# SBUF pools moved to two sides, rounded operands behind a 32-byte pad, in a two-block transformer kernel

## Chip, cores and metric

The kernel runs on one core of a Trainium2 chip, in one launch. The metric is device time in microseconds (us), the median of several runs. It holds two transformer blocks on 256 tokens with a model width of 1024, all in float32.

## What is computed

The first block normalises `x`, projects it, runs two attentions side by side (differential attention and a low-rank latent attention), gates and merges them, and adds a SwiGLU feed-forward layer. The second block does this twice: feed-forward, a mixer (retention the first time, stick-breaking attention the second), feed-forward, and a gated embedding. Nearly all the work is products with weight matrices:

```python
h = rms_norm(x, ln_mix_pre); z = h @ w_in
...                                   # two attentions on slices of z
merged = sigmoid(g_a) * (oa @ w_proj_a) + sigmoid(g_b) * (ob @ w_proj_b)
x = x + rms_norm(merged @ w_o, ln_mix_post)
x = x + rms_norm((silu(h @ w_gate) * (h @ w_up)) @ w_down, ln_ffn_post)
...                                   # second block, for i in (0, 1):
h = h + 0.5 * rmsnorm(swiglu(rmsnorm(h), gate, up, down))
h = h + rmsnorm(retention(rmsnorm(h)) if i == 0 else stick_breaking(rmsnorm(h)))
h = h + 0.5 * rmsnorm(swiglu(rmsnorm(h), gate, up, down))
h = h + rmsnorm(sigmoid(rmsnorm(h) @ ple_w_gate) * (p[i] @ ple_w_proj))
```

## The kernel before

**Rounded pairs.** Each float32 operand of a weight product is split into a rounded high part and a rounded rest, both of type float32r, and a product is three matmuls: high by high, high by rest, rest by high. `chunk` (line 161) loads up to 2048 columns of weights into a `w_raw` tile (a DMA on SP's queue, line 176), ScalarE rounds them into `w_hi` in pieces of 512 columns (line 188) and VectorE subtracts to get `w_lo` (line 189). A 512-column piece is 2,048 bytes in each partition. The activations are kept the same way: `x_hi` and `x_lo` (the input of a stage), `a_hi` and `a_lo` (the hidden layer of a feed-forward stage), `oa`, `ob`, `m` (the attention outputs and their merge), `u` (retention), `o` (stick-breaking), `pe` (the embedding input).

**Which operand moves.** A matmul has a stationary operand of 128 columns, loaded first, and a moving operand that streams past it. In `mm3` (line 192, its matmuls recorded as line 197), which `tokens` and `token_steps` call, the activation is stationary and 512 columns of weights move; one activation tile serves as `x[0]`, `x[0]`, `x[1]`, so a triple reads the high tile twice and the low tile once as stationary operands. In `mat_steps` (matmuls recorded as line 214) it is the other way round: 128 weight columns are stationary and 256 token columns of the activation move. The trace writes a matmul as out<-moving,stationary.

**Stages.** `first` runs the first block's mixer; `ffn` runs gate and up (activation `x`) and then, through `end_stage`, down (activation `a`, 22 row tiles, 2 token halves, 2 column halves: 88 triples for each of 5 stages). TensorE executes in program order; the loads run ahead over 3 `w_raw` buffers and 12 buffers each of `w_hi` and `w_lo`.

**Where tiles lie.** SBUF memory is given out by pools. A pool takes a stretch of every partition when it opens and gives it back when it closes; the tiles in it are rounded up to 32 bytes. All pools here are on the left side: they are stacked upwards from byte 16,512 of the partition in the order in which they open. From the tiles' sizes the places are: `const` 16,512, `raw` 20,448, `hip` (all `w_hi`) 45,024, `lop` (all `w_lo`) 69,600, `act` 94,176 with `h` first (8,192 bytes), `x_hi` at 102,368 and `x_lo` at 110,560, then `sm` 118,752 and `tmp` 123,008. `ob_hi` and `ob_lo` take the places of `x_hi` and `x_lo` (same tags in `act`). Above, from 136,320, come the pools that live for a stage: `mix` (with `oa`, `va`, `vb`, `m`, `cq`, `ckv`), `big0`, then `p_halves` (for good), and on top of it `big0a`, `ret_u` and `ret`, `emb0` and `big0b` and so on.

**Remainders of these places.** Divided by 64, the places of `w_raw`, `w_hi`, `w_lo`, `h`, `x` and `ob` leave 32. All the tiles in the stage pools (`a`, `u`, `oa`, `m`, `o`, `pe`, `cq`, `ckv`, and retention's `p` and `v`) leave 0. Divided by 512, `w_hi`, `w_lo`, `x` and `ob` leave 480 and the stage tiles named leave 128. Slices inside a tile start at multiples of 512 bytes, so every operand of a float32r weight product has its tile's remainder.

Of the kernel before, what the change touches and what calls it, by code (L numbers as in the profile page):

```python
# [10 lines left out]
F32 = mybir.dt.float32  # L11
# [7 lines left out]
P = 128  # L19
T = 256  # L20
D = 1024
# [73 lines left out]
class Weights:  # L95


    def __init__(self):
        self.parts = []
# [45 lines left out]
class Build:  # L145
    def __init__(self, ctx, tc, aps):
        self.ctx, self.tc, self.nc = ctx, tc, tc.nc
        self.aps = aps
        self.plan = []
        self.at = 0  # L150
        pool = lambda name, bufs, **k: ctx.enter_context(tc.tile_pool(name=name, bufs=bufs, **k))
        self.const = pool("const", 1)
        self.raw = pool("raw", 3)
        self.hip = pool("hip", WB)
        self.lop = pool("lop", WB)
        self.act = pool("act", 1)
        self.sm = pool("sm", 2)
        self.tmp = pool("tmp", 2)
        self.psm = pool("psm", 4, space=PSUM)
        self.psa = pool("psa", 4, space=PSUM)  # L160
        self.filler, self.behind, self.late = Filler(), None, []
        self.later = None
# [337 lines left out]

    def setup(self):
        nc, const, aps = self.nc, self.const, self.aps
        self.h = self.act.tile([P, 2, D], F32, name="h", tag="h")

        self.h0 = self.h.rearrange("p b d -> p (b d)").rearrange("p (k t) -> p k t", k=KT)
        self.vecs = const.tile([P, NV], F32, name="vecs")
        self.kc = const.tile([P, NK], F32, name="kc")
        nc.scalar.dma_start(self.kc[:, :P], aps["kc"][:, :P])
        nc.scalar.dma_start(self.vecs[:, :KT], aps["vecs"][:, :KT])
        self.pos = self.tmp.tile([P, T], I32, name="pos", tag="s")  # L510
        self.lam = self.tmp.tile([P, 4 * 64], F32, name="lam", tag="s")
        self.ident = self.kc[:, K_ID : K_ID + P]
        self.ones = const.tile([P, P], F32, name="ones")
        nc.vector.memset(self.ones, 1.0)
        self.dummies(WARM[0])
        self.mhalf = const.tile([P, 2], F32, name="mhalf")
        nc.vector.memset(self.mhalf, -0.5)
# [777 lines left out]
    def run(self):  # L1295
        tc = self.tc
        self.setup()
        g2 = lambda i, n: self.vec(V_G2 + (i * 8 + n) * 8, 8)
        row = lambda i, n: R_G2 + 4 * i + n // 2
        stage = self.first()  # L1300
        with tc.tile_pool(name="big0", bufs=1) as self.big:
            self.ffn(*stage, ("w_ffn_gate", "w_ffn_up", "w_ffn_down"), (0,), R_FFN, 1.0)
        names = ("ffn_w_gate_2", "ffn_w_up_2", "ffn_w_down_2")
        out = self.aps["out"].rearrange("p (b d) -> p b d", b=2)
        p_halves = self.ctx.enter_context(tc.tile_pool(name="p_halves", bufs=1))
        self.pe = [p_halves.tile([P, SUB], F32R, name=f"pe_{x}") for x in "hl"]
        pos = self.tmp.tile([P, T], I32, name="pos", tag="s")
        self.nc.gpsimd.dma_start(pos, self.aps["pos2"].to_broadcast([P, T]))
        self.table2 = self.rope_table("2", pos, self.kc[:, K_F2 : K_F2 + 1], self.const)
        for i in range(2):  # L1310
            with tc.tile_pool(name=f"big{i}a", bufs=1) as self.big:
                self.ffn(*self.next_stage(g2(i, 0)), names, (i, 0), row(i, 1), 4.0)
            self.later = lambda i=i: self.embed_in(i)
            mixer = self.stick if i else self.retention
            mixer(*self.next_stage(g2(i, 2)), row(i, 3))
            with tc.tile_pool(name=f"emb{i}", bufs=1) as emb:
                e = emb.tile([P, 2, D], F32, name="e")
                self.embed(i, e)
                with tc.tile_pool(name=f"big{i}b", bufs=1) as self.big:
                    self.ffn(*self.next_stage(g2(i, 4)), names, (i, 1), row(i, 5), 4.0)  # L1320
                self.ple(i, *self.next_stage(g2(i, 6), 4.0), e, row(i, 7), out if i else None)
        assert self.at == WCOLS * P, (self.at, WCOLS * P)
# [66 lines left out]
```

## Time and profile before

| | |
|---|---|
| median of 3 runs | 1613.9 us (1613.33 to 1614.34) |
| the profiled execution, its own time | 1613.39 us |
| its span (first to last instruction) | 1611.5 us |
| mean granted TensorE clock | 0.998 |
| TensorE matmul, weight load | 99%, 83% of the span |
| VectorE, ScalarE, GpSimd | 66%, 56%, 5% of the span |

The profile is one execution of the program. In its lists PE is TensorE's matmuls and PEld its loads of stationary operands, which overlap the matmuls; DVE is VectorE, ACT ScalarE, POOL GpSimd, SP the queue that issues most DMAs. The duration of a matmul in a list runs until its last result is written, so matmuls that follow each other overlap; the time one costs is read from start to start. The order of the work is on TensorE's queue, so the profile is read in three steps: the chain of work that ended last, the list of groups, and then single stages in order of time.

### The profile page before, as it was taken

How to read it: one execution, taken by the hardware profiler on the slowest of the kernel's cores; microseconds unless marked ns; L12 is line 12 of the kernel's file. 1: busy time of each engine (PE TensorE's matmuls, PEld its weight loads, DVE VectorE, ACT ScalarE, POOL GpSimd, SP SyncE). 2: the span in 40 equal slices, each digit the busy share in tenths (PEclk: the TensorE clock that was granted, in tenths of full speed). 3: DMA queues.
4: the chain of work that ended last, by engine and by line, in shares of the span. 5: the costliest groups of instructions: out<-in, count | busy, mean ns of one | idle time of the engine just before them, and what ended most of it. 6: DMA issues, size and time to landing. Idle time of an engine off the chain costs nothing.

```text
span 1611.5 us, 22515 instructions
## 1 busy us (share of the span) xinstructions
PE 1597.7 (99%) x8230; PEld 1344.3 (83%) x8230; DVE 1065.2 (66%) x1969; ACT 904.1 (56%) x1792; POOL 79.9 (5%) x97
## 2 busy tenths in 40 slices
PE   9999999999999999999999999999999999999997
PEld 8898778888888888898888888878888899888886
DVE  7987766765566665777766555486665677666546
ACT  6665544755455554645546555476554656655545
POOL 0000000200001000100000000012000200000001
PEclk9999999999999999999999999999999999999999
DMA  7535436455546555555455555555555554455552
GB/s 243 211 123 190 167 106 221 183 179 201 183 159 220 183 183 183 167 189 183 160 190 179 187 178 188 183 198 200 183 183 183 176 192 149 165 183 183 183 175 73
DMA packets 47134, 288.72 MB, mean 179 GB/s; under 512 B 5968, under 2 KB 9168, under 8 KB 14384
## 3 DMA queue, kind: packets, MB, share of 16 engines
q1 hardware_dynamic: 44528, 279.29, 49.3%
q0 software_dynamic: 2064, 7.80, 1.4%
q8 instruction: 64, 1.05, 0.3%
q14 instruction: 46, 0.38, 0.1%
q10 hardware_dynamic: 432, 0.20, 0.0%
HBM read 284.78 MB, written 1.05 MB: 177 GB/s over the span
## 4 chain that ended last, share of the span: by engine, by line
PE 95%; DVE 2%; DMA 1%; issue 1%; ACT 1%; SPq 0%; POOL 0%; POOLq 0%; DVEq 0%; ACTq 0%
PE ps L197 78%; PE ps L214 9%; PE at L628 1%; PE S L660 1%; PE xt L429 1%; DMA w_raw<-in_w 1%; DVE w_lo L189 1%; PE o L197 1%; PE o L707 0%; DMA h<-in_x 0%; PE S L1073 0%; PE S L1187 0%; PE pt L697 0%; PE o L834 0%; PE ot L1110 0%
## 5 line engine op out<-in xcount | busy, mean ns | idle before, releaser
L189 DVE TENSOR_TENSOR w_lo<-w_raw,w_hi 128x512 fp32r<-128x512 f32 x1054 | 708.8, 687 | 348.8 <-ACT w_hi L188 343.5
L188 ACT CAST w_hi<-w_raw 128x512 fp32r<-128x512 f32 x1054 | 639.6, 621 | 489.2 <-PE ps L197 355.8
L197 PE MATMUL ps<-w_hi,x_hi 128*128 128x512 f32 (+1 forms) x1280 | 488.9, 382 | 0.3 <-ACT x_hi L433 0.3
L197 PE MATMUL ps<-w_hi,x_lo 128*128 128x512 f32 (+1 forms) x1280 | 483.0, 377 | 0.5 <-DVE x_lo L435 0.5
L197 PE MATMUL ps<-w_lo,x_hi 128*128 128x512 f32 (+1 forms) x1280 | 482.1, 377 | 0.0
L197 PEld LDWEIGHTS ps<-w_hi,x_lo 128*128 128x128 f32 x1280 | 240.8, 188 | 46.9 <-DVE x_lo L435 2.1
L197 PEld LDWEIGHTS ps<-w_hi,x_hi 128*128 128x128 f32 x1280 | 241.0, 188 | 43.3 <-issue 1.0
L197 PEld LDWEIGHTS ps<-w_lo,x_hi 128*128 128x128 f32 x1280 | 241.2, 188 | 42.1
L197 PE MATMUL ps<-w_hi,a_hi 128*128 128x512 f32 x440 | 176.7, 402 | 0.0
L197 PE MATMUL ps<-w_hi,a_lo 128*128 128x512 f32 x440 | 173.3, 394 | 0.0
L197 PE MATMUL ps<-w_lo,a_hi 128*128 128x512 f32 x440 | 172.6, 392 | 0.0
L296 POOL TENSOR_TENSOR r<-v,mhalf 128x1 f32<-128x1 f32 (+1 forms) x50 | 61.4, 1228 | 1262.6 <-DVE v L384 1097.7
L214 PE MATMUL ps<-x_hi,w_hi 128*128 128x256 f32 x440 | 114.8, 289 | 0.7 <-ACT x_hi L356 0.5
L214 PE MATMUL ps<-x_hi,w_lo 128*128 128x256 f32 x440 | 112.5, 284 | 0.6 <-DVE w_lo L189 0.6
L197 PEld LDWEIGHTS ps<-w_hi,a_lo 128*128 128x128 f32 x440 | 82.6, 188 | 21.3
L197 PEld LDWEIGHTS ps<-w_lo,a_hi 128*128 128x128 f32 x440 | 82.7, 188 | 19.2
L197 PEld LDWEIGHTS ps<-w_hi,a_hi 128*128 128x128 f32 x440 | 82.6, 188 | 18.4
L214 PEld LDWEIGHTS ps<-x_hi,w_hi 128*128 128x128 f32 x440 | 84.0, 191 | 2.2 <-issue 0.7
L214 PEld LDWEIGHTS ps<-x_hi,w_lo 128*128 128x128 f32 x440 | 84.1, 191 | 1.5 <-DVE w_lo L189 1.2
L623 DVE SCALAR_TENSOR_TENSOR a<-ps,R,s 128x512 f32<-128x512 f32 (+1 forms) x60 | 42.2, 703 | 55.4 <-PE ps L197 44.0
L214 PE MATMUL ps<-x_lo,w_hi 128*128 128x256 f32 x440 | 77.4, 283 | 0.0
L270 ACT CAST a_hi<-at 128x512 fp32r<-128x512 f32 (+1 forms) x60 | 33.1, 551 | 70.4 <-PE at L628 70.4
(271 smaller groups left out, 1484.0 us busy)
## 6 DMA issues: line engine op xcount, KB each, us to landing
w_raw<-in_w SPq DMA_DIRECT2D x254, 1024.0 KB, 4.9
gr<-in_rows POOLq DMA_DIRECT2D x10, 512.0 KB, 4.1
w_raw<-in_w SPq DMA_DIRECT2D x7, 512.0 KB, 3.4
w_raw<-in_w SPq DMA_DIRECT2D x12, 256.0 KB, 5.1
w_raw<-in_w SPq DMA_DIRECT2D x6, 384.0 KB, 3.3
h<-in_x SPq DMA_DIRECT2D x4, 256.0 KB, 5.6
h<-in_x POOLq DMA_DIRECT2D x1, 1024.0 KB, 8.9
out<-h SPq DMA_DIRECT2D x3, 256.0 KB, 2.5
```

Of the source, the lines that this page charges most:

```text
L188: nc.scalar.copy(hi[:, :m], r[:, c0:c1])
L189: nc.vector.tensor_sub(lo[:, :m], r[:, c0:c1], hi[:, :m].bitcast(F32))
L197: mm = lambda a, b, **k: nc.tensor.matmul(ps, a, b, skip_group_check=True, **k)
L214: mm = lambda *a, **k: self.nc.tensor.matmul(*a, skip_group_check=True, **k)
L270: nc.scalar.copy(hi, src)
L296: self.nc.gpsimd.tensor_tensor(r, v, self.mhalf[:, :n], op=ALU.pow)
L429: nc.tensor.transpose(pt[:, i, :], self.h[:, b, k * P : (k + 1) * P], self.ident)
L623: nc.vector.scalar_tensor_tensor(a, banks[1], R[:, b : b + 1], s, op0=ALU.mult, op1=ALU.mult)
L628: nc.tensor.transpose(pt[:, i, :], a[:, i * P : (i + 1) * P], self.ident)
L660: mm(S[:, at], q[:, qs], k[:, ks], start=n == 0, stop=n == len(parts[0]) - 1, skip_group_check=True)
```

## The change

Pools get a side. `const`, `raw`, `sm`, `tmp`, later `p_halves` and `emb0`/`emb1` go to the right side, where pools are stacked downwards from byte 229,344; `h` moves out of `act` into a pool `res` of its own on the right. On the left a pool `pad` with one tile of 8 floats (32 bytes) opens first, so that `hip`, `lop`, `act` and the stage pools are stacked from byte 16,544. No instruction on any engine is written, removed or given other shapes; the pad is never read or written.

```diff
-        self.const = pool("const", 1)
-        self.raw = pool("raw", 3)
+
+        self.const = pool("const", 1, side="right")
+        self.raw = pool("raw", 3, side="right")
+        pool("pad", 1).tile([P, 8], F32, name="pad")
         self.hip = pool("hip", WB)
         self.lop = pool("lop", WB)
         self.act = pool("act", 1)
-        self.sm = pool("sm", 2)
-        self.tmp = pool("tmp", 2)
+        self.res = pool("res", 1, side="right")
+        self.sm = pool("sm", 2, side="right")
+        self.tmp = pool("tmp", 2, side="right")
...
-        self.h = self.act.tile([P, 2, D], F32, name="h", tag="h")
+        self.h = self.res.tile([P, 2, D], F32, name="h", tag="h")
...
-        p_halves = self.ctx.enter_context(tc.tile_pool(name="p_halves", bufs=1))
+        p_halves = self.ctx.enter_context(tc.tile_pool(name="p_halves", bufs=1, side="right"))
...
-            with tc.tile_pool(name=f"emb{i}", bufs=1) as emb:
+            with tc.tile_pool(name=f"emb{i}", bufs=1, side="right") as emb:
```

## Rows read from the trace of the kernel before

**Rows 1.** The page's head: span, and each engine's busy time.

```profile
span 1611.5 us, 22515 instructions
PE 1597.7 (99%) x8230; PEld 1344.3 (83%) x8230; DVE 1065.2 (66%) x1969; ACT 904.1 (56%) x1792; POOL 79.9 (5%) x97
```

**Rows 2.** The page's chain that ended last, shares by engine and by line.

```profile
PE 95%; DVE 2%; DMA 1%; issue 1%; ACT 1%; SPq 0%; POOL 0%; POOLq 0%; DVEq 0%; ACTq 0%
PE ps L197 78%; PE ps L214 9%; PE at L628 1%; PE S L660 1%; PE xt L429 1%; DMA w_raw<-in_w 1%; DVE w_lo L189 1%; PE o L197 1%; PE o L707 0%; DMA h<-in_x 0%; PE S L1073 0%; PE S L1187 0%; PE pt L697 0%; PE o L834 0%; PE ot L1110 0%
```

**Rows 3.** Timeline, TensorE, a gate/up stage: start us, duration us, matmul.

```profile
339.75 0.39 PE L197 MATMUL ps<-w_hi,x_hi 128*128 128x512 f32 x1
...
349.95 0.39 PE L197 MATMUL ps<-w_hi,x_hi 128*128 128x512 f32 x1
```

**Rows 4.** Timeline, TensorE, the down stage that follows it.

```profile
429.75 0.40 PE L197 MATMUL ps<-w_hi,a_hi 128*128 128x512 f32 x1
429.99 0.39 PE L197 MATMUL ps<-w_lo,a_hi 128*128 128x512 f32 x1
430.22 0.39 PE L197 MATMUL ps<-w_hi,a_lo 128*128 128x512 f32 x1
...
439.55 0.40 PE L197 MATMUL ps<-w_hi,a_hi 128*128 128x512 f32 x1
```

**Rows 5.** Timeline, TensorE, end of the second attention's projection and start of w_o.

```profile
261.54 0.39 PE L197 MATMUL ps<-w_hi,ob_hi 128*128 128x512 f32 x1
...
263.58 0.39 PE L197 MATMUL ps<-w_hi,ob_hi 128*128 128x512 f32 x1
...
268.65 0.39 PE L197 MATMUL ps<-w_hi,m_h 128*128 128x512 f32 x1
...
271.45 0.39 PE L197 MATMUL ps<-w_hi,m_h 128*128 128x512 f32 x1
```

**Rows 6.** Timeline, TensorE, retention's output products of one head.

```profile
768.88 0.39 PE L197 MATMUL o<-v_l,p_h 128*128 128x512 f32 x1
...
769.58 0.39 PE L197 MATMUL o<-v_h,p_l 128*128 128x512 f32 x1
...
770.27 0.39 PE L197 MATMUL o<-v_h,p_l 128*128 128x512 f32 x1
```

**Rows 7.** Busy time of each engine in that down stage (PE, PEld, DVE, ACT, POOL; clock, DMA).

```profile
418.00:474.00 56.00, 56.00 (x242) 45.06 (x241) 27.97 (x42) 25.99 (x44) 0.55 (x1) 1.00 0.54 188
338.00:356.00 18.00, 18.00 (x81) 14.87 (x80) 10.12 (x15) 9.64 (x16) 0.00 (x0) 1.00 0.60 208
```

**Rows 8.** Groups of matmuls by shape: counts | busy us, mean ns | idle before.

```profile
L197 PE MATMUL ps<-w_hi,x_hi 128*128 128x512 f32 x1120 | 442.9, 395 | 0.3 <-ACT x_hi L433 0.3
L197 PE MATMUL ps<-w_hi,a_hi 128*128 128x512 f32 x440 | 176.7, 402 | 0.0
L197 PE MATMUL ps<-w_hi,u_h 128*128 128x512 f32 x64 | 25.1, 392 | 0.0
L197 PE MATMUL ps<-w_hi,m_h 128*128 128x512 f32 x32 | 12.7, 398 | 0.0
L197 PE MATMUL ps<-w_hi,pe_h 128*128 128x512 f32 x16 | 6.3, 392 | 0.0
L197 PE MATMUL o<-v_h,p_h 128*128 128x512 f32 x12 | 4.6, 421 | 0.0
L197 PE MATMUL ps<-w_hi,ckv_h 128*128 128x512 f32 x8 | 3.3, 408 | 0.0
L214 PE MATMUL ps<-x_hi,w_hi 128*128 128x256 f32 x440 | 114.8, 289 | 0.7 <-ACT x_hi L356 0.5 <-DVE h L774 0.2
L197 PE MATMUL ps<-w_hi,x_hi 128*128 128x256 f32 x160 | 46.0, 288 | 0.0
L214 PE MATMUL ps<-cq_h,w_hi 128*128 128x256 f32 x36 | 9.9, 296 | 0.0
```

**Rows 9.** Timeline, TensorE, 256-column matmuls, moving operand x, then cq.

```profile
681.45 0.28 PE L214 MATMUL ps<-x_hi,w_hi 128*128 128x256 f32 x1
...
682.89 0.28 PE L214 MATMUL ps<-x_hi,w_hi 128*128 128x256 f32 x1
...
165.79 0.28 PE L214 MATMUL ps<-cq_h,w_hi 128*128 128x256 f32 x1
...
167.90 0.28 PE L214 MATMUL ps<-cq_h,w_hi 128*128 128x256 f32 x1
```

**Rows 10.** Groups by shape: the two largest of the transposes.

```profile
L628 PE MATMUL at<-kc,a 128*128 128x128 f32 x220 | 33.7, 271 | 0.0
L429 PE MATMUL xt<-kc,h 128*128 128x128 f32 x144 | 19.9, 274 | 0.5 <-DVE h L415 0.5
```

**Rows 11.** Groups by shape, VectorE: the subtraction that makes w_lo.

```profile
L189 DVE TENSOR_TENSOR w_lo<-w_raw,w_hi 128x512 fp32r<-128x512 f32 x1042 | 702.7, 689 | 348.2 <-ACT w_hi L188 342.9
```

## Prediction

> **What bounds the kernel now.** First read the page's head: matmuls keep TensorE busy for 1597.7 of 1611.5 us, VectorE 66%, ScalarE 56% [rows 1]. Then the chain that ended last: TensorE holds 95% of it, and 78% is one line, the 512-column matmuls of line 197 [rows 2]. So a wait removed on another engine is worth almost nothing here; what counts is how long TensorE takes from one matmul to the next. The change alters no instruction, only where operands lie. So the third look is at single stages, from start to start, and the question is whether that time already differs between places.
>
> It does. In a gate/up stage 45 matmuls start between 339.75 and 349.95: 10.20 us, 0.680 a triple, 227 ns each [rows 3]. In the down stage that follows, same line, same shapes, 42 matmuls take from 429.75 to 439.55: 9.80 us, 0.700 a triple, 233 ns each [rows 4]. Both run at a granted clock of 1.00 (the 2.4 GHz level), and TensorE never goes idle in either stretch [rows 7], so neither clock nor starvation makes the difference. The stationary operand does differ: `x` leaves 32 divided by 64, `a` leaves 0. A cleaner pair: near the end of the second attention's projection, with `ob` in `x`'s place, 9 matmuls take 2.04 us (0.680 a triple); just after, in w_o, with `m` in a stage pool, 12 take 2.80 us (0.700) [rows 5]. Line, moving buffers, shapes and neighbours in time are alike; only the stationary tile's place is another. And it isn't that stationary and moving tile must match: retention's `p` and `v` both leave 128 divided by 512, and six of their matmuls take 1.39 us, 232 ns each [rows 6], nearer to 233 than to 227, though six are few. So I read a stationary operand's place as costing 6.7 ns a matmul (20 ns a triple) where it leaves 0.
>
> **Where everything goes.** By the pools' sizes: on the left the pad at 16,512, `w_hi` from 16,544, `w_lo` from 41,120, `x_hi` 65,696, `x_lo` 73,888, the stage pools from 82,080. Every tile of rounded operands on the left is a multiple of 512 bytes long, so all of them there leave 160 divided by 512, 32 divided by 64. `a`, `u`, `oa`, `m`, `o`, `cq`, `ckv`, `p` and `v` thus go from 0 to 32; `w`, `x`, `ob` stay at 32. On the right: `const` 225,408 (each constant keeps its remainder by 64), `raw` 200,832 (32 becomes 0), `h` 192,640 (32 becomes 0), `tmp` 175,072, `p_halves` 170,976 (0 becomes 32), `emb` 162,784. The largest stage pool, `mix`, ends at 169,120, so all fits.
>
> **The gain.** Triples whose stationary operand leaves 0 today: 440 with `a`, 64 with `u`, 32 each with `oa`, `m` and `o` (the row of `m` stands for three), 16 with `pe`, 12 with `p`, 8 with `ckv` [rows 8]: 636. At 0.700 - 0.680 = 0.020 us that is 12.7 us. The load that costs is, as I read it, that of the next matmul's stationary operand, so where another kind of matmul follows (a transpose after a triple, at the ends of runs) nothing is gained; I take off 0.3 us for some 45 such places: 12.4.
>
> Does it reach the end? These stages are TensorE back to back. In 56 us of a down stage VectorE is busy 27.97 and ScalarE 25.99 us, DMA 0.54 [rows 7]; a stage 3% shorter asks 3% more of each, and the gate/up stage already runs at the faster pace with VectorE at 10.12 of 18 us. So all of it.
>
> **The losses.** As moving operand `cq` (remainder 0) is a little faster today than `x` (32): 18 matmuls of 256 columns in 2.11 us, 117 ns, against 12 in 1.44 us, 120 ns [rows 9]. `cq` (3 x 36 matmuls) and `ckv` (3 x 16) go to 32: 156 x 2.8 ns = 0.4 us lost. Transposes: 220 of `a` last 271 ns, 144 of `h` 274 ns [rows 10], and the two swap remainders: (220 - 144) x 3 ns = 0.2 us at most, either way; I take 0. The float32 matmuls of the attentions are not told apart by any row; their lines hold some 2% of the chain [rows 2], 32 us, and 3% of that (what 20 ns is of 0.700 us) is 1 us either way; I take 0.
>
> `w_raw` changes its remainder, which could change ScalarE's rounding or VectorE's subtraction (689 ns [rows 11]) and the DMA's writes; no row shows either at another place. VectorE, the busier of the two, has a third of its time free [rows 1], so its subtraction could be a third longer (10.12 us would become some 13 of 18 [rows 7]) before TensorE waited: 0. If that cover went, the price would be set by the stage: every per cent by which VectorE outlasted TensorE is a per cent of that stage. At the start, some 40 us fed by DMA, and where stages change, a shifted place may release a buffer sooner or later: `emb`'s tile no longer shares memory with the stage before it. In the chain DMA and VectorE together hold 3%, 48 us [rows 2], so a tenth of that, 5 us, bounds it both ways; nothing waits on `e` on the chain, I take 0.
>
> Sum: 12.4 - 0.4 = 12.0 us. The profiled execution took 1613.39 us (its span 1611.5, 1.9 around it), 0.5 below the median of 1613.9. 1613.39 - 12.0 = 1601.4; on the median's scale 1601.9. I forecast 1602.
>
> **What the Trainium skill says against it.** "TensorE: Matmul & The Clock Gate", section "Step-by-step: what each phase is for", says that TensorE has two independent SBUF read ports, so that loading the next weights doesn't steal read bandwidth from the running matmul. By that rule the place of the stationary operand is worth nothing and the sum is 0; the trace disagrees by the 20 ns a triple above. "SBUF — State Buffer", in its box on SBUF cachelines, tells of 16-byte lines; every tile here starts on such a line before and after, so by it nothing changes either.
>
> **Rivals.** *Slower: the step that decides is not 64.* The trace knows two remainders by 512 for stationary operands, 480 (fast) and 128 (slow). After the change all have 160, which no row shows. Slices of `x` lie 512 bytes apart and all run at 227 ns [rows 3], so steps over 512 are out; but 64, 128, 256 or 512 may be the one that counts. By 128 the fast remainder is 96, the slow 0, the new one 32. If 160 counts as slow, the places now slow stay so, and those now fast lose 6.7 ns: 3 x 1120 matmuls with `x` and 96 with `ob` [rows 8] are 23.0 us, and 3 x 440 + 3 x 160 of 256 columns with a `w` or an `x` loaded [rows 8], at the same 6.7 ns, 12.0 us. 1613.4 + 35 = 1648. It decides as soon as over a third of this bites (12.4 of 35). The same price follows if the pad took no room, since 16,512 leaves 0.
>
> *Not the remainder but the height.* All slow stationary tiles lie above 136,000, the fast ones below 119,000. After the change all but `pe` lie lower (`a` from 82,080), so this gives the same gain less 48 x 6.7 ns = 0.3 us: 1602 again. It speaks for the forecast, not against.
>
> *Same: the difference belongs to the stages, not to the place* (the skill's rule above would say so). 1613.4. Against it: `ob` and `m`, side by side [rows 5]. *Much faster:* 160 could also be better than 480, by as much as the slow one is worse: 1602 - 35 = 1567.
>
> **Chances.** Of five readings (64, height, 128, 256, 512) two give the forecast and three leave 160 open; I count the open ones half, and 64 somewhat more, as it is the one by which moved and unmoved tiles come out alike. Forecast, 1597 to 1611: 0.72. Much faster: 0.03. Same: 0.08. Slower: 0.17. A measurement can tell about 0.2% (3 us) from no change. Range: the low end is the forecast less the 5 us of stage changes, 1597; the high end takes in the same case, 1614.5. Faster 0.75, same 0.08, slower 0.17.
>
> **What would show it.** Right: down-stage triples from 0.700 to 0.680 (42 matmuls in 9.52 us instead of 9.80), `u`, `m`, `o`, `oa` too, gate/up triples still 0.680, other engines' times unchanged, the order of instructions the same. Wrong: gate/up triples at 0.700 (the slower rival), down triples still 0.700 (the same case), or TensorE waiting for `w_lo` in places where it doesn't now.

## The result, and the profile after

The changed kernel takes 1603.4 us (median of 4 runs, 1603.2 to 1603.6), against 1613.7 before: a ratio of 0.9936, with a 95% interval of 0.9918 to 0.9953, 10.3 us less. Forecast were 1602 and 12.0 us less. The gain came where it was forecast, in the matmuls of the down stages and their like. The reason given for it was wrong, the right number came partly by luck, and the pad has no part in it.

The page's head and chain after, to be read beside [rows 1, 2]:

```profile
span 1601.5 us, 22514 instructions
PE 1587.1 (99%) x8230; PEld 1345.8 (84%) x8230; DVE 1064.0 (66%) x1969; ACT 904.1 (56%) x1792; POOL 79.8 (5%) x97
...
PE 96%; DVE 1%; DMA 1%; ACT 1%; issue 1%; SPq 0%; POOL 0%; POOLq 0%; DVEq 0%; ACTq 0%
```

The span is 10.0 us shorter and TensorE is busy 10.6 us less. The counts of compute instructions are the same, TensorE's matmuls come in the same order, and VectorE (1.2 us less) and ScalarE have the times they had: the difference is on TensorE. Line numbers are 3 higher.

The timeline of TensorE after, first the gate/up stage, then the down stage, then the same 256-column matmuls as before (start us, duration us):

```profile
338.76 0.39 PE L200 MATMUL ps<-w_lo,x_hi 128*128 128x512 f32 x1
...
349.64 0.39 PE L200 MATMUL ps<-w_lo,x_hi 128*128 128x512 f32 x1
...
428.80 0.39 PE L200 MATMUL ps<-w_hi,a_hi 128*128 128x512 f32 x1
...
438.32 0.39 PE L200 MATMUL ps<-w_hi,a_hi 128*128 128x512 f32 x1
...
678.15 0.28 PE L217 MATMUL ps<-x_hi,w_hi 128*128 128x256 f32 x1
...
679.59 0.28 PE L217 MATMUL ps<-x_hi,w_hi 128*128 128x256 f32 x1
```

The gate/up stage runs as before: 16 triples in 10.88 us, 0.680 each [rows 3]. The down stage now does 14 triples in 9.52 us, 0.680 each, where it took 9.80 [rows 4]. The short matmuls take 1.44 us for 12, as before [rows 9].

One activation stayed slow, and it is the row that broke the theory. Timeline after, the embedding's product:

```profile
865.28 0.40 PE L200 MATMUL ps<-w_hi,pe_l 128*128 128x512 f32 x1
865.52 0.40 PE L200 MATMUL ps<-w_hi,pe_h 128*128 128x512 f32 x1
865.75 0.39 PE L200 MATMUL ps<-w_lo,pe_h 128*128 128x512 f32 x1
865.98 0.40 PE L200 MATMUL ps<-w_hi,pe_l 128*128 128x512 f32 x1
```

Three matmuls, 0.70 us. Yet `pe` now lies at 170,976 and leaves 32 divided by 64, the remainder that was to be the fast one. What sets it off from `a`, `u` and `m` is that it went to the right side: it leaves 480 divided by 512, its weights 160.

### The profile page after: what moved, and what is told of

Its sections match the earlier page's. It is cut to its first block, busy times and chain, and to the rows that moved or that the text cites. A ratio compares the mean times of both kernels' runs of the same rounds, so it can differ in the third digit from the quotient of the medians.

```text
span 1601.5 us, 22514 instructions
## 1 busy us (share of the span) xinstructions
PE 1587.1 (99%) x8230; PEld 1345.8 (84%) x8230; DVE 1064.0 (66%) x1969; ACT 904.1 (56%) x1792; POOL 79.8 (5%) x97
## 4 chain that ended last, share of the span: by engine, by line
PE 96%; DVE 1%; DMA 1%; ACT 1%; issue 1%; SPq 0%; POOL 0%; POOLq 0%; DVEq 0%; ACTq 0%
PE ps L200 79%; PE ps L217 10%; PE S L663 2%; PE at L631 1%; PE xt L432 1%; DMA w_raw<-in_w 1%; PE o L200 1%; PE o L710 0%; PE o L837 0%; PE S L1076 0%; PE S L1190 0%; PE pt L700 0%; ACT w_hi L191 0%; DVE w_lo L192 0%; PE ot L1113 0%
## 5 line engine op out<-in xcount | busy, mean ns | idle before, releaser
L200 PE MATMUL ps<-w_hi,a_hi 128*128 128x512 f32 x440 | 172.7, 393 | 0.0
```

The costliest lines, as they stand in the source:

```text
L200: mm = lambda a, b, **k: nc.tensor.matmul(ps, a, b, skip_group_check=True, **k)
```

## The experiments

Below, the *distance* is the place of the stationary operand less that of the moving one, divided by 256, remainder taken. Theory A is the prediction's (the stationary operand's own remainder by 64); theory B says that the two operands must agree, which is distance 0. No trace carries an address: all places are worked out from the sizes of the pools' tiles.

**The changed kernel without its pad.**

```diff
-        pool("pad", 1).tile([P, 8], F32, name="pad")
```

> The changed kernel without the pad: all rounded operands on the left leave 128 divided by 512 (0 by 64), and moving and stationary agree. Theory A (the stationary operand's own remainder by 64 decides, 32 fast, 0 slow): triples at 0.700 us in all stages, gate/up too, about 1603 + 12 + 35 = 1650 us. Theory B (moving and stationary operand must leave the same remainder by 128 or 512, whatever it is): triples stay at 0.680, 1603 us. Theory C (they must agree and leave 32 by 64): as A, 1650 us.

It took 1603.1 us. Its timeline, gate/up and down:

```profile
338.38 0.39 PE L199 MATMUL ps<-w_hi,x_hi 128*128 128x512 f32 x1
...
347.91 0.39 PE L199 MATMUL ps<-w_hi,x_hi 128*128 128x512 f32 x1
...
430.03 0.39 PE L199 MATMUL ps<-w_hi,a_hi 128*128 128x512 f32 x1
...
439.55 0.39 PE L199 MATMUL ps<-w_hi,a_hi 128*128 128x512 f32 x1
```

14 triples in 9.53 and in 9.52 us: 0.680 each, with all operands leaving 0 divided by 64. Theory A is dead, and so is C, which wanted agreement and a remainder of 32 by 64 at once. B stands: the operands agree.

**The changed kernel, activations 64 bytes off the weights.**

```diff
+        pool("pad2", 1).tile([P, 16], F32, name="pad2")
         self.act = pool("act", 1)
```

> The changed kernel with 64 more bytes ahead of the activations' pools: weights stay at 160 divided by 512 (32 by 128), activations go to 224 (96 by 128); both still leave 32 by 64. Theory A (own remainder by 64): nothing changes, 0.680 a triple, 1603 us. Theories B and C (moving and stationary must agree by 128 or more): they disagree in every weight product, 0.700 a triple everywhere, about 1650 us.

It took 1629.7 us. The timeline of a gate/up stage, and of the 256-column matmuls:

```profile
344.97 0.39 PE L201 MATMUL ps<-w_hi,x_hi 128*128 128x512 f32 x1
...
355.47 0.39 PE L201 MATMUL ps<-w_hi,x_hi 128*128 128x512 f32 x1
...
687.63 0.28 PE L218 MATMUL ps<-x_hi,w_hi 128*128 128x256 f32 x1
...
689.04 0.28 PE L218 MATMUL ps<-x_hi,w_hi 128*128 128x256 f32 x1
```

15 triples in 10.50 us, 0.700 each, in the stage that had been at 0.680 throughout; both operands still leave 32 divided by 64. So agreement it is. The time is 20 us under the expected 1650. For the most part that is the 256-column matmuls, which did not slow down with the others: 12 of them take 1.41 us instead of 1.44. They gained from the distance that costs the long ones time, so the 12 us counted for them did not come and 2.4 us came back (summed over the trace, against the kernel before). The rest is the long ones with `x` and `ob`: they lost 16.9 us, not 23.

**The kernel before, one pad below the stage pools: 32 bytes, then 96.**

```diff
         self.tmp = pool("tmp", 2)
+        pool("pad", 1).tile([P, 8], F32, name="pad")    # [P, 24] for 96 bytes
```

> The kernel before, all pools on the left, with a pad of 32 bytes after tmp, so that only the stage pools move: a, u, m, o, oa, pe leave 160 divided by 512 (32 by 128), the weights stay at 480 (96 by 128), and the stage tiles stay above byte 136,000. Theory A (own remainder by 64): down-stage triples fall from 0.700 to 0.680, about 1602 us. Theories B and C (agreement by 128 or more): they stay at 0.700, about 1614 us. A theory of height (low fast, high slow): 0.700, 1614 us.

> The kernel before with a pad of 96 bytes after tmp: the stage tiles leave 224 divided by 512 (96 by 128) and the weights 480 (96 by 128): they agree by 128, not by 512, at heights above 136,000. Theory A (own remainder by 64): 0.680 in the down stages, about 1602 us. Theories B and C with agreement by 128: the same, 1602 us; with agreement by 512: 0.700, 1614 us. Height: 0.700, 1614 us. With the run of the 32-byte pad it tells agreement (fast here, slow there) from the own remainder (fast in both) and from height (slow in both).

They took 1606.2 and 1602.3 us. A down stage of each, 32 bytes first:

```profile
430.18 0.39 PE L198 MATMUL ps<-w_hi,a_hi 128*128 128x512 f32 x1
...
439.79 0.39 PE L198 MATMUL ps<-w_hi,a_hi 128*128 128x512 f32 x1
```

```profile
430.24 0.39 PE L198 MATMUL ps<-w_hi,a_hi 128*128 128x512 f32 x1
...
439.76 0.39 PE L198 MATMUL ps<-w_hi,a_hi 128*128 128x512 f32 x1
```

14 triples in 9.61 us (0.686) and in 9.52 us (0.680). With 96 bytes the operands agree by 256 but not by 512 (224 and 480), and the time is the fast one: 256 is enough, and height plays no part, since `a` still lies above 136,000. Here `pe` agrees with the weights too, and its triples take 0.680 (median). With 32 bytes the distance is 192 and the cost lies between: none of the theories had a middle. Distance 192 isn't distance 64, so the pattern doesn't repeat by 128. And with 96 bytes a single line, without moving any pool to the other side, has the whole gain.

**A map of the other distances**, on the changed kernel without its pad.

```diff
+        pool("pad2", 1).tile([P, 32], F32, name="pad2")
         self.act = pool("act", 1)
...
+        self.big.tile([P, 40], F32, name="pad_a")       # before a_hi, a_lo
+            up.tile([P, 24], F32, name="pad_u")         # before u_h, u_l
+            sp.tile([P, 104], F32, name="pad_o")        # before o_h, o_l
```

> The changed kernel without the pad, weights at 128 divided by 256, with pads that give each activation another distance to the weights (stationary less moving place, divided by 256): x, ob, m and oa 128, a and o 32, u 224. So far 0 gave 0.680 us a triple, 64, 96 and 160 gave 0.700, 192 gave 0.687. Theory D (the distance of the two operands by 256 decides, worst in the middle): x and m at 0.700, a at 0.680 to 0.700, u at 0.680 to 0.687; with x slow about 1603 + 23 = 1626 us, less what the 256-column matmuls give back. Theory E (the distance by 128 decides, and 192 is an exception): x and m at 0.680, u near 0.700 (224 is 96 by 128), a at 0.700 (32 is 160 by 128), about 1613 us. Theory A (own remainder by 64, already against the runs): x, a, o and u all leave 0 or 32 by 64 and would be told apart by that alone: x 0 slow, u and a 32 fast.

It took 1627.9 us. The timeline for `x` (128), `a` (32) and `u` (224):

```profile
344.75 0.39 PE L200 MATMUL ps<-w_hi,x_hi 128*128 128x512 f32 x1
...
355.20 0.40 PE L200 MATMUL ps<-w_hi,x_hi 128*128 128x512 f32 x1
...
435.28 0.40 PE L200 MATMUL ps<-w_hi,a_hi 128*128 128x512 f32 x1
...
445.77 0.40 PE L200 MATMUL ps<-w_hi,a_hi 128*128 128x512 f32 x1
...
850.04 0.39 PE L200 MATMUL ps<-w_hi,u_h 128*128 128x512 f32 x1
...
860.54 0.40 PE L200 MATMUL ps<-w_hi,u_h 128*128 128x512 f32 x1
```

15 triples each: 0.697, 0.699 and 0.700 us. Theory D had `u` near the fast end and was wrong there; E had `x` fast and was wrong there. With the other runs the map by 256 is: 0: 0.680; 32: 0.699; 64: 0.700; 96: 0.702 (`pe` in this run and the one without the pad, medians of few triples); 128: 0.697; 160: 0.700; 192: 0.686; 224: 0.700. It isn't a smooth valley: agreement is fast, 192 is two thirds of the way back, everything else costs about 17 to 22 ns a triple.

**The rests 64 bytes off the high tiles**, on the kernel before: pads so that `w_hi`, `x_hi`, `a_hi` and their like leave 224 divided by 256, and `w_lo`, `x_lo`, `a_lo` and their like 32.

```diff
+        pool("pad_w", 1).tile([P, 16], F32, name="pad_w")
         self.lop = pool("lop", WB)
+        pool("pad_x", 1).tile([P, 48], F32, name="pad_x")
         self.act = pool("act", 1)
...
+        pool("pad_s", 1).tile([P, 8], F32, name="pad_s")    # below the stage pools
...
+    # 64 bytes between the high tile and the rest of x, a, u, oa, m, o, cq, ckv and pe
```

> The kernel before with pads so that all high tiles (weights and activations) leave 224 divided by 256 and all rests 32: 64 bytes off. In 512-column triples the load that runs beside a moving tile is always high beside high or rest beside rest, so every distance is 0. Theory D: all triples 0.680 as in the 96-byte pad's run; in the 256-column matmuls two of three pairs (high beside rest) are now 64 apart, and at 64 and 192 apart these took 118 ns against 120, so some 1300 x 2 ns = 2.6 us less: about 1600 us. If a 256-column matmul doesn't care (rival: the 118 came with the whole stage being slower paced elsewhere), 1602.3 as the 96-byte pad's run. Were it not the tile loaded beside a moving one that counts but the one just multiplied with it, the second and third of a triple would be 64 apart: 0.693 a triple, about 1613 us.

A miss: 1617.9 us. The timeline of a down stage:

```profile
429.92 0.40 PE L201 MATMUL ps<-w_hi,a_hi 128*128 128x512 f32 x1
...
439.62 0.40 PE L201 MATMUL ps<-w_hi,a_hi 128*128 128x512 f32 x1
```

14 triples in 9.70 us, 0.693. So it isn't only the load running beside a matmul that must agree with its moving operand. The last reading named had the 0.693, but at 1613 us, and with the second and third matmul of a triple slow. From start to start the first takes 233 ns, the second 232 and the third 229 (medians over the five down stages): the slowest is the one whose own two operands agree. So that reading isn't borne out either.

**Only a_lo 64 bytes off**, on the kernel with the 96-byte pad.

```diff
-        A = [self.big.tile([P, FF, T], F32R, name=f"a_{x}", tag=f"a{x}") for x in ("hi", "lo")]
+        A = [self.big.tile([P, FF, T], F32R, name="a_hi", tag="ahi")]
+        self.big.tile([P, 16], F32, name="pad_a")
+        A.append(self.big.tile([P, FF, T], F32R, name="a_lo", tag="alo"))
```

> The 96-byte pad on the kernel before, and in the feed-forward stages 64 bytes between a_hi and a_lo: only a_lo stands 64 by 256 off the weights. In a triple (w_hi with a_hi, w_lo with a_hi, w_hi with a_lo) the load of a_lo runs beside the second matmul and is multiplied in the third. Reading N (what counts is the load running beside a matmul): the second takes 233 ns, first and third 227. Reading O (what counts is the stationary tile a matmul is multiplied with): the third takes 233, first and second 227. Either way 0.687 a triple, 440 triples x 7 ns = 3 us over the 96-byte pad's 1602.6: 1605.6. Reading X (a matmul suffers for both, or for the change of place from one to the next): second and third at 231 to 233, 0.691 to 0.693, about 1608.

It took 1607.6 us. Timeline:

```profile
430.40 0.39 PE L198 MATMUL ps<-w_lo,a_hi 128*128 128x512 f32 x1
430.63 0.40 PE L198 MATMUL ps<-w_hi,a_lo 128*128 128x512 f32 x1
430.87 0.39 PE L198 MATMUL ps<-w_hi,a_hi 128*128 128x512 f32 x1
431.10 0.39 PE L198 MATMUL ps<-w_lo,a_hi 128*128 128x512 f32 x1
431.33 0.40 PE L198 MATMUL ps<-w_hi,a_lo 128*128 128x512 f32 x1
...
432.02 0.40 PE L198 MATMUL ps<-w_hi,a_lo 128*128 128x512 f32 x1
```

Two triples from 430.63 to 432.02: 1.39 us, 0.69 each (0.693 over the five stages). One tile out of place in three costs 13 of the 20 ns. From start to start the first matmul of a triple takes 228 ns, the second 229, the third, the one with `a_lo`, 236 (medians over the five stages). Reading N is out: the second, beside which `a_lo` is loaded, hardly suffers. Reading O had 233 for the third alone: the place is right, the size isn't. X had the total, but not how it is spread. Together with the preceding experiment no rule for the single matmul comes out: there the third was the fastest, here it is the slowest, and in both it multiplies with a tile 64 off.

**Four versions, timed in one series** against the kernel before (1613.45 us): the 96-byte pad, the changed kernel without its pad, and two that use what the second experiment showed. There the long matmuls' operands agree, and the weights that are stationary in `mat_steps` lie 64 or 192 bytes further, in tiles 256 bytes longer (one scratch buffer of 512 bytes gives way for the room):

```diff
-            hi = self.hip.tile([P, SUB], F32R, name="w_hi", tag="a")
-            lo = self.lop.tile([P, SUB], F32R, name="w_lo", tag="b")
+            hi = self.hip.tile([P, SUB + 64], F32R, name="w_hi", tag="a")[:, off : off + SUB]
+            lo = self.lop.tile([P, SUB + 64], F32R, name="w_lo", tag="b")[:, off : off + SUB]
...
-            W = self.chunk([(name, lead, k, cols) for k in ks for name, lead, cols in specs], each)
+            W = self.chunk([(name, lead, k, cols) for k in ks for name, lead, cols in specs], each, 16)  # 48
```

> The kernel before with a pad of 96 bytes after tmp, timed: all float32r operands agree by 256, pools on one side, one line changed. If agreement is the whole of the change's gain: ratio to before 0.993, the same as or up to 1 us below the changed kernel's 1603.4 (in whose first 36 us TensorE came 1.1 us later than before). If the two sides gave something of their own: above 1603.4.

> The changed kernel without its pad, timed: every rounded operand on the left leaves 128 by 512, all agree. If only agreement counts, the pad is worth nothing: 1603.2 to 1603.5, as the changed kernel. If 32 by 64 has any worth of its own, slower by more than 1 us.

> The 96-byte pad on the kernel before (all operands of 512-column triples leave 224 by 256), and the weights of mat_steps, which are stationary there, lie 64 bytes further in tiles that are 256 bytes longer. So the 512-column triples stay at 0.680 us, and in the 256-column matmuls of mat_steps stationary less moving place is 64 by 256. If the distance that costs the long matmul time gives the short one time back (cq at 64 took 114 ns against 120 in the run of the 32-byte pad): 1320 to 1476 matmuls x 2 to 6 ns, 3 to 9 us less than the 96-byte pad's 1602.3: 1594 to 1599 us. If the short matmul's gain came only with cq's two pairs a step, or with the tiles it follows: 1602.

> As the kernel with 64 bytes, with 192 instead: the 256-column matmuls of mat_steps at 192 by 256, where x and w took 118 ns against 120 in the run with 64 bytes ahead of the activations: 1476 x 2 ns, 3 us less than the 96-byte pad's 1602.3, 1599 us. If the short matmul doesn't care about the distance: 1602.

| version | median us (lowest to highest) | ratio to before, 95% interval |
|---|---|---|
| 96-byte pad, one side | 1602.6 (1601.8 to 1603.5) | 0.9932 (0.9918 to 0.9947) |
| changed kernel, no pad | 1602.3 (1601.7 to 1602.7) | 0.9930 (0.9915 to 0.9945) |
| 96-byte pad, 64 bytes in mat_steps | 1599.7 (1599.5 to 1600.0) | 0.9914 (0.9898 to 0.9931) |
| 96-byte pad, 192 bytes in mat_steps | 1600.9 (1600.1 to 1601.8) | 0.9922 (0.9907 to 0.9936) |

The first two are one time, within about 1 us of what was expected: the two sides and the pad give nothing beyond agreement. The third takes 2.9 us less than the 96-byte pad, just short of the 3 to 9 expected, and 3.8 less than the changed kernel (timed in another series). The fourth takes 1.7 us less than the pad where 3 were expected, and its slowest run is as slow as the pad's fastest: a gain hardly clear of the spread, though its trace has 118 ns where the pad's has 120. The 256-column matmuls of the third, with `x` moving, then with `cq`:

```profile
677.79 0.28 PE L215 MATMUL ps<-x_hi,w_hi 128*128 128x256 f32 x1
...
679.20 0.28 PE L215 MATMUL ps<-x_hi,w_hi 128*128 128x256 f32 x1
...
163.87 0.28 PE L215 MATMUL ps<-cq_h,w_hi 128*128 128x256 f32 x1
...
165.23 0.28 PE L215 MATMUL ps<-cq_h,w_hi 128*128 128x256 f32 x1
```

12 in 1.41 us (117.5 ns) against 1.44, and for `cq` 12 in 1.36 us (113 ns).

## Why the prediction came out right

**What bounds, and where.** Right. TensorE is 96% of the chain, its matmuls come in the same order, and the 20 ns that two stages of the old trace showed was the whole of the matter: the down stages went from 0.700 to 0.680, as the forecast's own test asked.

**The reason.** Wrong, and the step can be named: the sentence that stationary and moving tile need not match, drawn from six matmuls of retention [rows 6]. There `p` and `v` have distance 0 and took 1.39 us. With that sentence agreement was ruled out, and the operand's own remainder was left. Rows 3 to 5 fit both readings equally: `x` and `ob` agreed with the weights, `a` and `m` were 160 off. The six were too few, and too near an interruption. Only two matmuls lie between them and two others of retention that took 341 and 238 ns from start to start, and behind such an interruption operands that agree run slow as well. The gate/up stage of [rows 3] shows it, ahead of those rows, where it begins behind transposes:

```profile
337.57 0.48 PE L197 MATMUL ps<-w_hi,x_hi 128*128 128x512 f32 x1
...
338.36 0.40 PE L197 MATMUL ps<-w_hi,x_hi 128*128 128x512 f32 x1
```

From 338.36 to the first of [rows 3] at 339.75, six matmuls take 1.39 us, 232 ns each, exactly as in retention, though `x` agrees with the weights. The triples from 337.57 on take 0.784, 0.691, 0.697 and 0.684 us and then 0.680 each. The down stage never comes to that pace: 0.780, then 0.700 from the second triple on. So what a pair of operands costs can be read only some triples after an interruption.

The same six matmuls after the change, at the same distance 0:

```profile
765.45 0.39 PE L200 MATMUL o<-v_l,p_h 128*128 128x512 f32 x1
...
766.81 0.39 PE L200 MATMUL o<-v_h,p_l 128*128 128x512 f32 x1
```

1.36 us, 227 ns each. Weights, `p` and `v` now all agree, but that doesn't explain the difference by itself. In the changed kernel without its pad, where `p`, `v`, `x` and the weights all agree, two heads differ:

```profile
727.46 0.39 PE L199 MATMUL o<-v_l,p_h 128*128 128x512 f32 x1
...
728.84 0.39 PE L199 MATMUL o<-v_h,p_l 128*128 128x512 f32 x1
...
765.30 0.39 PE L199 MATMUL o<-v_l,p_h 128*128 128x512 f32 x1
...
766.67 0.39 PE L199 MATMUL o<-v_h,p_l 128*128 128x512 f32 x1
```

1.38 us in one head, 1.37 in the next. And in the second experiment, with the weights around them 64 off, one head's six take 1.36. What sets the pace of the first triples behind an interruption stays open.

By the wrong reason the forecast had the right sign, and that was luck: the new layout happens to fulfil both, as all tiles on the left have one remainder by 256 as well as 32 by 64. `pe` fulfils only the second and stayed at 0.700, where 0.3 us had been counted as gain.

**The sum.** 12.0 forecast, 10.0 between the two profiled executions. Summed over the traces from start to start, matmuls followed by one with `a` gave 8.2 us (8.8 expected: 440 x 20 ns), `u` 1.2 (1.3), `m` 0.6 (0.6), `o` 0.4 (0.6), `oa` 0.1 (0.6), `pe` 0 (0.3). The term most out of size is `oa`: its triples are cut through by the attentions' own matmuls, and their median stayed at 785 ns, far from 700. The loss of 0.4 on `cq` and `ckv` did not come: summed likewise, `cq` lost 0.2 us (its matmuls went from 117 to 120 ns as forecast), but `ckv`, waits included, gained 0.4.

The largest term off is the start. Both traces show it by the first reduction of the latent projection, here after:

```profile
49.32 1.39 PE L291 MATMUL ss<-ones,sqs 128*128 128x1 f32 x12
```

Before, it starts at 48.18: the first 50 us took 1.1 us longer, inside the 5 us left for such things. No run shows this to be a cost of the new layout: two executions of the changed kernel without its pad, with the same sides, reach this point at 48.05 and 48.87, and two of the 96-byte pad, with one side, at 47.12 and 47.71. So 0.6 to 0.8 us is what two executions of one kernel differ by. From there to the end the change gained 11.1 us.

**The rivals.** *Slower* was priced at 1648 for a layout in which everything disagrees. The second experiment is that layout: 1629.7. The price of a long matmul, 6.7 ns, is borne out by 0.700 a triple, but not the sum of 23 us: `x` and `ob` lost 16.9, since triples just behind an interruption were slow already and lost less (2 to 4 ns a matmul in the second to fourth triple, 6.7 from the seventh on). The 12 us for the short ones had the wrong sign, they gain 2 ns each. *Height* fell with the 96-byte pad. *Same* fell with the result, and *much faster* with the gate/up stage, which stayed at 0.680. That the trace showed no remainder like the new 160 was the right worry, and the map shows how it might have gone: a pad of 64 bytes a few lines lower costs 26 us.

**Against the Trainium skill.** "TensorE: Matmul & The Clock Gate", section "Step-by-step: what each phase is for", has loading the next weights take no read bandwidth from the running matmul. By that rule, as the prediction has it, the place of the stationary operand is worth nothing; the runs disagree by up to 20 ns a triple, and with the 96-byte pad only the stage pools had moved. Whether it is the load that holds up the running matmul isn't shown: with the rests 64 bytes off, each load agreed with the matmul running beside it, and a triple still took 0.693.

## What to carry to other kernels

Where TensorE is the bound, measure matmuls from start to start in each stage, and when two stages of one shape differ, compare the places of their operands with each other, not only with a boundary. Before a layout is changed by hand, a pad of 32, 64, 96 bytes at one point is a one-line experiment that shows what the whole change is worth; here one pad had all of it. And a row that rules out a reading must be as long as those it rules on, and as far from an interruption: six matmuls just behind one were not.

## What the runs showed that I had not expected

With float32r operands of 512 moving columns, in an unbroken run of triples, a matmul takes 227 ns from start to start when stationary and moving operand leave the same remainder divided by 256 (224, 160 and 128 occurred), and otherwise 229 to 234 ns, as the mean of a triple. Behind an interruption agreeing operands need up to about four triples, at 0.684 to 0.697 us, to come to that pace. With 256 moving columns the order is another: 120 ns in agreement, 118 at 64 or 192 bytes apart in the run with shifted activations, 113 for `cq` at 64. One tile of a triple out of place costs 13 of 20 ns, there most of it in the matmul that uses the tile (236 ns); with all rests out of place most falls on the other two (233 and 232). Why the short ones gain, why the pace takes some triples to settle, and what in TensorE's reading has a step of 256 bytes, stays open: no row shows the reads themselves.
